# Retention out of PSUM, a scheduler that knows the shared port, and reordered blocks in a hybrid attention and retention step

## The chip, the cores and the metric

One core of a Trainium2 chip runs the whole step in one launch. The metric is the device time in microseconds (us) of an execution, as the median of several. The engines are TensorE (PE; its weight loads are PEld), VectorE (DVE), ScalarE (ACT), GpSimd (POOL) and the DMA queue that SyncE (SP) feeds. SBUF is the on-chip memory; PSUM holds the matmuls' results in banks.

## What is computed

There are 1152 tokens: 128 context tokens and 1024 latent ones, of width 1024. One layer modulates its normalised input by a condition, projects it into attention and retention operands, runs both branches, gates, merges and projects out. Cut to what matters:

```python
mod = silu(cond) @ w_mod + b_mod
shift, scale, gate = split(mod, 3)
h = layernorm(x) * (1 + scale) + shift
qa, ka, va, za, qr, kr, vr, zr = split(h @ w_in)          # 8 heads of 2 x 64 / 128, 8 heads of 64 / 128
# differential attention, per head, with rotary on latent q and k, context keys ahead
oa = (softmax(q1 k1^T / 8) - lam * softmax(q2 k2^T / 8)) @ v
oa = rmsnorm(oa) * subln_g * (1 - lam_init);  oa = (oa * silu(za)) @ w_pa
# retention, per head, once forward and once backward over chunks of 128 tokens
inner = (q k^T) * decay_in                                # inside a chunk
o = inner @ v + (q @ s) * q_dec                           # s: state from the chunks before
s = s * chunk_dec + (k * k_dec)^T @ v                     # the recursion
orr = layernorm(o_fwd + o_bwd) * ret_gn_g;  orr = (orr * silu(zr)) @ w_pr
g = sigmoid(h @ w_gate + b_gate)
out = (g_a * oa + g_r * orr) @ w_out
y = layernorm(alpha * x + gate * out) * ln_g + ln_b
```

Outputs are y for both kinds of token, the context's keys and values, and the context's final retention states.

## The kernel before

The work is laid out in stages that follow one another on every engine. A head stage (to about 100 us) computes the modulation and `Y`, the modulated input, split into a rounded high part and a low part, so that three matmuls at a time make one exact product. Stage A (to about 645 us) runs the dense projections for q, k and v of both branches (`dn` banks) while `core()` runs retention; stage B (to 1345 us) runs the softmax of the attention while the other projections and gates serve as filler; stage D (to 1648 us) projects both branches; stage E multiplies by `w_out` and normalises the output, in nine blocks of 128 tokens and two halves of 512 columns.

Within a stage, one program writes the instructions of all engines, and class `Sched` sets in which order. It keeps a clock `t` for PE, advanced by each matmul's price in `mm` (L133), and a time for each of ACT, DVE and POOL, advanced in `op` (L54) by a price per operation (`act`, `v_tt`, `v_ts`, `v_stt`, `p_tt`, `p_ts`). Streams are generators that yield the time at which their next operands will be ready; `run` (L104) asks the streams in order and lets the first that is ready issue, and dense matmuls fill what is left. The order is thus fixed when the kernel is built; each engine's instructions then run in that order and wait for one another on semaphores.

Retention, `core()` at L761: per pair of heads, PE transposes the keys, and DVE scales them into `KD`. Per head, nine matmuls give U, the chunks' updates, in three PSUM banks of the pool `a` (of four); ACT copies U to SBUF; DVE runs the recursion `SS` over seven chunks, one `scalar_tensor_tensor` forward on 64 partitions and one backward on the other 64 at each (L157). POOL makes `QD`, the decayed queries. `inner` (L818): PE multiplies q and k, DVE multiplies by the decay `DT` into `inn`. `outp` (L827): PE adds `inn` times v and `QD` times `SS` in a bank, ACT copies it to `osb`, DVE takes statistics (`stt`, `mvr`). Then POOL makes `rstd`, `norm` (L858) normalises `osb` in place on DVE, PE transposes it, and ACT copies the result to `on`. Beside all that, the projections of q and k go through the rotation: DVE makes `sw` and `rt` out of `dn`, POOL and DVE finish `rt`, ACT and POOL or DVE split it into `qkh` and `qkl`. ACT and POOL also split each weight tile into `whi` and `wlo`.

`decays()` at L652 runs at the start of `core()`: it loads the decay parameters `dec` in five small loads, `kx` and `lp`, and computes `lg`, `kdec` and `DT` from them on DVE and ACT. `phase_h` (L332) loads the modulation's weights: `wm` with a row block at a time and `wk`. `softmax_stream` (L985) first waits until `sch.t + 8`, then issues score tiles `S`; DVE takes the maximum `nm`, ACT the exponential `E`. `out_stream` (L1406) issues the blocks of stage E in order, both halves of one before the next.

Of the kernel before, what the change touches and what calls it, by code (L numbers as in the profile page):

```python
# [18 lines left out]
P = 128  # L19
# [18 lines left out]
class Sched:  # L38
# [6 lines left out]
    def __init__(self):  # L45
        self.t = 0.0
        self.e = {"act": 0.0, "dve": 0.0, "pool": 0.0}
        self.q = []
# [78 lines left out]
def hybrid_step(ctx: ExitStack, tc: tile.TileContext, I: dict, O: dict):  # L127
# [5 lines left out]
    def mm(out, lhsT, rhs, start, stop):  # L133
        n = rhs.free_size()
        sch.t += max(n / 2400, 0.107) if lhsT.dtype == F32R else max(n / 600, 0.214)
        nc.tensor.matmul(out, lhsT=lhsT, rhs=rhs, start=start, stop=stop)  # L136

    def tpose(out, in_):
        sch.t += 0.107
        nc.tensor.transpose(out, in_, ident)  # L140
# [5 lines left out]

    def v_tt(out, a, b, op, after=None):
        nc.vector.tensor_tensor(out, a, b, op=op)  # L148
        return sch.op("dve", 0.07 + out.free_size() / 960, after)

    def v_ts(out, a, s1, s2, op0, op1=None, after=None, fast=False):
        kw = {} if op1 is None else {"op1": op1}
        nc.vector.tensor_scalar(out, a, s1, s2, op0=op0, **kw)  # L153
        return sch.op("dve", 0.12 + out.free_size() / (1920 if fast else 960), after)
# [13 lines left out]
    def p_tt(out, a, b, op, after=None):  # L168
        nc.gpsimd.tensor_tensor(out, a, b, op=op)  # L169
        return sch.op("pool", 0.2 + out.free_size() * (0.17 if op == ALU.pow else 0.00205), after)  # L170

    def p_ts(out, a, s1, op0, after=None):
        nc.gpsimd.tensor_scalar(out, a, s1, None, op0=op0)  # L173
        return sch.op("pool", 0.2 + out.free_size() * 0.0013, after)
# [155 lines left out]


    def phase_h(first):  # L332
# [3 lines left out]
        with es:  # L336
# [144 lines left out]
            for k in range(0, KT, 2):  # L481
                load_wk(1, k)
            by_rows("scale", 0)
# [74 lines left out]
    def phase_a():  # L558
        es_ps = ExitStack()
        psum_pool(es_ps, "a", 4)  # L560
# [78 lines left out]
        last_parts = phase_h(first)  # L639
# [12 lines left out]
        def decays():  # L652
            rd = I["ret_decay"]
            dec = pa.tile([P, 32], F32, name="dec")
            dma(dec[:, 0:16], rd.rearrange("d h -> (d h)").partition_broadcast(P))
            rp = rd.rearrange("d (q two) -> two d q", two=2)
            for r in range(2):
                dst = dec[r * 64:(r + 1) * 64, 16:24].rearrange("p (d q) -> p d q", d=2)
                dma(dst, rp[r].partition_broadcast(64))
                dma(dec[r * 64:(r + 1) * 64, 24:32], rd[r].partition_broadcast(64))  # L660
            kx = pa.tile([P, 16], F32, name="kx")
            dma(kx, I["ret_kexp"])
            lp = pa.tile([P, 4, 64], F32, name="lp")
            dma(lp, I["lam_params"].partition_broadcast(P))
# [96 lines left out]
        def core():  # L761
# [3 lines left out]
            for p in range(4):  # L765
# [17 lines left out]
                for e in range(2):  # L783
# [8 lines left out]
                    U = pa.tile([P, NTILE, P], F32, tag="U", name="U")  # L792
# [6 lines left out]
                    for g0, gn in GR:  # L799
                        yield room("a")  # L800
                        ups, tok = psum("a", (P, 4, P))
                        for i in range(gn):
                            c = g0 + i
                            mm(ups[:, i, :], KD[e][:, c].rearrange("p d k -> p (d k)"), vr[:, c, vs], True, True)
                        tok[0] = act(U[:, g0:g0 + gn, :], ups[:, :gn, :])
                    dma(O["st"][h], U[:, NTILE - 1, :])
                    s_f = tok[0]
                    for c in range(NCH - 1):
                        b = NCH - 1 - c
                        fw, bw = (s0[0:64, :], s0[64:128, :]) if c == 0 else (SS[0:64, c, :], SS[64:128, b, :])  # L810
                        v_stt(SS[0:64, c + 1, :], fw, g128[0:64, h:h + 1], U[0:64, c, :], ALU.mult, ALU.add, s_f)
                        s_f = v_stt(SS[64:128, b - 1, :], bw, g128[64:128, h:h + 1], U[64:128, b, :], ALU.mult, ALU.add)
# [3 lines left out]
                    mv = pa.tile([P, NTILE, 2], F32, tag="mvr", name="mvr")  # L816

# [9 lines left out]
                    def outp(g0, gn, t, _):  # L827
# [7 lines left out]
                        f = act(osb[:, g0:g0 + gn, :], ops[:, :gn, :])  # L835
                        for i in range(gn):
                            v_bn(stt[:, g0 + i, :], ops[:, i, :], f)
                            nc.vector.bn_aggr(mv[:, g0 + i, :], stt[:, g0 + i:g0 + i + 1, :])
                            f2 = sch.op("dve", 0.08)
                        tok[0] = max(f, f2)  # L840
                        return f2
# [93 lines left out]
    def phase_b():  # L935
# [49 lines left out]
        def softmax_stream():  # L985
            n = 0
            yield sch.t + 8.0
# [418 lines left out]
        def out_stream():  # L1406
            for i in range(NTILE):
                ts = slice(i * P, (i + 1) * P)
# [9 lines left out]
                st, mv, rs = sm[:, 0:12].rearrange("p (g s) -> p g s", g=2), sm[:, 12:14], sm[:, 14:15]  # L1418
                for g in range(2):
                    gs = slice(g * 512, (g + 1) * 512)  # L1420
                    yield room("e")
                    ps, tok = psum("e")
                    for k in range(KT):
                        mm(ps, X[k][:, 0, ts], Y[:, 0, k, gs], k == 0, False)
                        mm(ps, X[k][:, 0, ts], Y[:, 1, k, gs], False, False)
                        mm(ps, X[k][:, 1, ts], Y[:, 0, k, gs], False, k == KT - 1)
                        if k % 2:
                            yield 0
                    tok[0] = v_tt(y[:, gs], ps, gl[:, gs], ALU.mult)
                    v_stt(y[:, gs], xt[:, gs], ALPHA, y[:, gs], ALU.mult, ALU.add)  # L1430
                    f = v_bn(st[:, g, :], y[:, gs])
# [3 lines left out]
                def fin(i=i, y=y, mv=mv, rs=rs):  # L1435
# [6 lines left out]
                sch.later(f, fin, "y")  # L1442
            done["E"] = True
# [125 lines left out]
```

## Time and profile before

| what | value |
|---|---|
| median of three runs | 1761.46 us (1760.38 to 1763.36) |
| the profiled execution's own time | 1763.77 us |
| its span | 1761.8 us |
| mean granted clock of PE | 0.981 |
| PE busy | 1676.1 us, 95% of the span |
| DVE, ACT, POOL busy | 902.6, 621.9, 819.3 us |
| moved by DMA | 237.36 MB, 135 GB/s in the mean |

The span is the profiled execution from its first to its last instruction; 2.0 us of its time lie around it. Busy time counts what an engine executes; that PE is busy says neither at which clock nor whether a matmul waited for its operands within its own record. [...]

### The profile page before, as it was taken

The page shows a single profiled execution, that of the slowest core. Times are in us where ns is not written, and L with a number is a line of the kernel's source. Part 1 is how long each engine was busy: PE and PEld are TensorE (multiplying, and loading weights), DVE is VectorE, ACT ScalarE, POOL GpSimd, SP SyncE. Part 2 cuts the span into 40 slices and gives each one's busy share as a digit, 9 for nine tenths or more (in the row PEclk, how much of TensorE's full clock was granted, in tenths as well). Part 3 has the DMA queues.
Part 4 walks back from the last instruction along what each step waited for, and adds up shares of the span by engine and source line. Part 5 has one row for each costly group of instructions (what it writes and reads, how often), then busy time and mean ns, then how long its engine had stood idle before and what let it go on. Part 6 is the DMA issues. An engine that isn't in the chain of part 4 may idle for free.

```text
span 1761.8 us, 27014 instructions
## 1 busy us (share of the span) xinstructions
PE 1676.1 (95%) x10471; PEld 1621.6 (92%) x10471; DVE 902.6 (51%) x1675; ACT 621.9 (35%) x1163; POOL 819.3 (47%) x553
## 2 busy tenths in 40 slices
PE   6989999899899989999999999999999999999997
PEld 4789899899899879999999999999999999999786
DVE  8636606612742744656565556556655013234666
ACT  5532212322222224545555555554555220012200
POOL 4636415532552645767466746575755332112211
PEclk8999999999999989999999999999999999999999
DMA  8245322330230254353535353535342568754422
GB/s 300 85 121 142 100 70 66 105 128 24 96 120 24 95 170 149 125 185 113 158 104 163 99 162 98 161 98 157 99 150 81 200 231 275 257 179 139 163 101 90
DMA packets 135040, 237.36 MB, mean 135 GB/s; under 512 B 15784, under 2 KB 103040, under 8 KB 133888
## 3 DMA queue, kind: packets, MB, share of 16 engines
q1 hardware_dynamic: 134912, 235.63, 41.4%
q8 instruction: 83, 1.36, 0.3%
q14 instruction: 45, 0.37, 0.1%
HBM read 161.08 MB, written 74.49 MB: 134 GB/s over the span
## 4 chain that ended last, share of the span: by engine, by line
PE 71%; DVE 12%; DMA 7%; issue 4%; POOL 3%; ACT 2%; SPq 1%; POOLq 0%; DVEq 0%; ACTq 0%
PE dn L136 45%; PE S L136 8%; PE o L136 5%; PE e L136 5%; PE tp L140 4%; DVE SS L157 3%; PE a L136 3%; DMA gt<-Gd 3%; DVE junk L157 2%; DMA gt<-ONd 1%; DVE osb L153 1%; SPq L187 1%; DMA lp<-in_lam_params 1%; DVE sw L598 1%; PE tp L136 1%
## 5 line engine op out<-in xcount | busy, mean ns | idle before, releaser
L136 PE MATMUL dn<-Y,whi 128*128 128x384 f32 x3200 | 837.3, 342 | 5.2 <-DVE rt L148 3.1
L136 PEld LDWEIGHTS dn<-Y,whi 128*128 128x128 f32 x3200 | 569.0, 190 | 11.3 <-DVE rt L148 4.0
L136 PE MATMUL dn<-Y,wlo 128*128 128x384 f32 x1600 | 538.1, 336 | 0.0
L169 POOL TENSOR_TENSOR wlo<-raw,whi 128x1024 fp32r<-128x1024 f32 x87 | 209.6, 2412 | 477.7 <-ACT whi L143 477.0
L136 PEld LDWEIGHTS dn<-Y,wlo 128*128 128x128 f32 x1600 | 302.2, 189 | 0.1
L1029 DVE TENSOR_REDUCE nm<-S 128x1 f32<-128x1152 f32 x144 | 178.2, 1237 | 187.3 <-PE S L136 187.2
L143 ACT ACTIVATE E<-S,nm 128x1152 f32<-128x1152 f32 x144 | 162.2, 1126 | 95.7 <-DVE nm L1029 95.4
L173 POOL TENSOR_SCALAR E<-E,r 128x640 f32<-128x640 f32 x64 | 146.4, 2287 | 93.2 <-DVE r L157 65.4
L136 PE MATMUL dn<-whi,Y 128*128 128x256 f32 x864 | 156.5, 283 | 9.5 <-DVE rt L148 7.9
L136 PEld LDWEIGHTS dn<-whi,Y 128*128 128x128 f32 x864 | 134.4, 190 | 10.5 <-ACT ln L143 8.2
L136 PE MATMUL o<-wTh,V 128*128 128x256 f32 x576 | 131.5, 287 | 0.0
L143 ACT ACTIVATE wTh<-tp 128x512 fp32r<-128x512 f32 (+1 forms) x168 | 89.5, 543 | 104.6 <-PE tp L140 103.9
L143 ACT ACTIVATE whi<-raw 128x1024 fp32r<-128x1024 f32 x88 | 91.9, 1053 | 87.3 <-PE dn L136 87.3
L136 PE MATMUL dn<-wlo,Y 128*128 128x256 f32 x432 | 121.2, 281 | 0.0
L136 PE MATMUL S<-K,QH 128*128 128x384 f32 (+1 forms) x400 | 97.2, 347 | 10.1 <-ACT E L143 6.1
L148 DVE TENSOR_TENSOR wTl<-tp,wTh 128x512 fp32r<-128x512 f32 (+1 forms) x168 | 98.1, 612 | 15.9 <-ACT wTh L143 15.9
L169 POOL TENSOR_TENSOR E<-E 128x640 f32<-128x640 f32 x64 | 100.2, 1565 | 5.3
L136 PEld LDWEIGHTS o<-wTh,V 128*128 128x128 f32 x576 | 99.2, 188 | 0.2
L136 PE MATMUL S<-K,QL 128*128 128x384 f32 (+1 forms) x400 | 93.5, 337 | 0.4 <-DMA QL<-Ql 0.4
L140 PE MATMUL tp<-ident,E 128*128 128x128 f32 x584 | 88.2, 272 | 1.8 <-DVE wTl L148 1.8
L153 DVE TENSOR_SCALAR KD<-tp,kdec 128x256 f32<-128x256 f32 (+1 forms) x48 | 16.0, 408 | 144.3 <-PE tp L140 144.3
L157 DVE SCALAR_TENSOR_TENSOR gt<-gt,dn 128x384 f32<-128x384 f32 x48 | 26.6, 554 | 120.8 <-DMA gt<-Gd 66.6
(201 smaller groups left out, 2594.4 us busy)
## 6 DMA issues: line engine op xcount, KB each, us to landing
K<-Kd SPq DMA_DIRECT2D x8, 1280.0 KB, 7.2
V<-Vd SPq DMA_DIRECT2D x24, 384.0 KB, 4.1
Gd<-gt SPq DMA_DIRECT2D x48, 192.0 KB, 2.1
gt<-Gd SPq DMA_DIRECT2D x48, 192.0 KB, 2.4
Y<-OAd SPq DMA_DIRECT2D x16, 576.0 KB, 4.9
raw<-in_w_gate SPq DMA_DIRECT2D x16, 512.0 KB, 4.8
QH<-Qh SPq DMA_DIRECT2D x64, 128.0 KB, 2.8
QL<-Ql SPq DMA_DIRECT2D x64, 128.0 KB, 2.9
```

Of the source, the lines that this page charges most:

```text
L136: nc.tensor.matmul(out, lhsT=lhsT, rhs=rhs, start=start, stop=stop)
L140: nc.tensor.transpose(out, in_, ident)
L143: nc.scalar.activation(out, in_, func, **kw)
L148: nc.vector.tensor_tensor(out, a, b, op=op)
L153: nc.vector.tensor_scalar(out, a, s1, s2, op0=op0, **kw)
L157: nc.vector.scalar_tensor_tensor(out, a, s, b, op0=op0, op1=op1, **kw)
L169: nc.gpsimd.tensor_tensor(out, a, b, op=op)
L173: nc.gpsimd.tensor_scalar(out, a, s1, None, op0=op0)
L187: nc.sync.dma_start(out=out, in_=in_)
L598: nc.vector.stream_shuffle(sw[:, :n], ps[:, :n], SWAP)
L1029: nc.vector.tensor_reduce(nm[:, m:m + 1], ps[:, :nb, :kw], axis=AX.XY, op=ALU.max, negate=True)
```

## The change

Six things are changed.

1. `Sched.op` models a port that DVE and POOL share: a DVE operation whose inputs lie in SBUF and a POOL operation don't overlap in the model; one waits for the other. PE's prices are raised a little.
2. The loads of `dec`, `kx` and `lp` are issued in `phase_h`, behind the second group of `wk` loads, into a pool of their own.
3. U stays in PSUM: the recursion reads the banks, which are held until it has ended. The context chunk's U alone is copied, to `ust`, which is stored. The order of the three groups is now the single one first.
4. The copy to `osb` is dropped: the statistics read the output banks, as before, and the norm reads them too and writes `osb`. The three banks are held until the norm has ended.
5. `softmax_stream` starts at `sch.t + 16`.
6. `out_stream` issues the first two blocks as first halves of both, then second halves of both.

The numbers of instructions are the same on PE, DVE, POOL and SP. ACT has 48 copies fewer (24 of U, 24 of `osb`) and 8 more (`ust`).

```diff
-    def op(self, eng, cost, after=None):
+    def op(self, eng, cost, after=None, port=False):
+
         s = max(self.e[eng], self.t + self.LAG if after is None else after)
+        if port:
+            other = "pool" if eng == "dve" else "dve"
+            mine, theirs = self.held[eng], self.held[other]
+            for a, b in theirs:
+                if a < s < b:
+                    s = b
+            mine.append((s, s + cost))
+            del mine[:-24]
+            if theirs and theirs[-1][0] >= s:
+                self.held[other] = [(a, b) if a < s else (a + cost, b + cost) for a, b in theirs]
+                self.e[other] += cost
         self.e[eng] = s + cost
...
-        sch.t += max(n / 2400, 0.107) if lhsT.dtype == F32R else max(n / 600, 0.214)
+        sch.t += max(n / 2400 + 0.013, 0.11) if lhsT.dtype == F32R else max(n / 600 + 0.01, 0.22)
...
+    def in_sbuf(*aps):
+        return all(a.tensor.space != PSUM for a in aps)
...
-        return sch.op("dve", 0.12 + a.free_size() / 960, after)
+        return sch.op("dve", 0.12 + a.free_size() / 960, after, in_sbuf(a, b))
...
             for k in range(0, KT, 2):
                 load_wk(1, k)
+            load_decays()
             by_rows("scale", 0)
...
-                    for g0, gn in GR:
+                    U, u_tok = {}, []
+                    for g0, gn in (GR[2], GR[0], GR[1]):
...
-                        tok[0] = act(U[:, g0:g0 + gn, :], ups[:, :gn, :])
-                    dma(O["st"][h], U[:, NTILE - 1, :])
-                    s_f = tok[0]
+                            U[c] = ups[:, i, :]
+                        if gn == 1:
+                            ust = pa.tile([P, P], F32, tag="ust", name="ust")
+                            tok[0] = act(ust, ups[:, 0, :])
+                            dma(O["st"][h], ust)
+                        else:
+                            u_tok.append(tok)
...
-                        v_stt(SS[0:64, c + 1, :], fw, g128[0:64, h:h + 1], U[0:64, c, :], ALU.mult, ALU.add, s_f)
+                        v_stt(SS[0:64, c + 1, :], fw, g128[0:64, h:h + 1], U[c][0:64], ALU.mult, ALU.add, s_f)
...
+                    for tok in u_tok:
+                        tok[0] = s_f
...
-                        f = act(osb[:, g0:g0 + gn, :], ops[:, :gn, :])
...
-                            normed[0] = v_ts(osb[:, c, :], osb[:, c, :], mv[:, c, 0:1], rstd[:, c:c + 1],
-                                             ALU.subtract, ALU.mult, fast=True)
+                            normed[0] = v_ts(osb[:, c, :], outs[c], mv[:, c, 0:1], rstd[:, c:c + 1],
+                                             ALU.subtract, ALU.mult)
+                        for tok in o_tok:
+                            tok[0] = normed[0]
...
-            yield sch.t + 8.0
+            yield sch.t + 16.0
...
+            order = [(0, 0), (1, 0), (0, 1), (1, 1)] + [(i, g) for i in range(2, NTILE) for g in range(2)]
+            for i, g in order:
+                if g == 0:
+                    begin(i)
+                yield from part(i, g)
```

Three places show how the instructions move. The helpers stand 16 lines lower now, so the same operation has another line number.

The first is SP's queue in the head stage. Before:

```order
L187 DMA wk<-in_w_scale_k 128x2x512 x4
L187 DMA wm<-in_w_shift 128x1024 x4
L187 DMA raw<-in_w_ka 128x1024
L187 DMA wm<-in_w_shift 128x1024
L187 DMA rc<-in_rope_c 128x1024
L187 DMA rsn<-in_rope_s 128x1024
L187 DMA raw<-in_w_vr 128x1024 x2
L187 DMA dec<-in_ret_decay 128x16
L187 DMA dec<-in_ret_decay 64x8x1
L187 DMA dec<-in_ret_decay 64x8
```

After:

```order
L203 DMA wk<-in_w_scale_k 128x2x512 x4
L203 DMA dec<-in_ret_decay 128x16
L203 DMA dec<-in_ret_decay 64x8x1
L203 DMA dec<-in_ret_decay 64x8
L203 DMA dec<-in_ret_decay 64x8x1
L203 DMA dec<-in_ret_decay 64x8
L203 DMA kx<-in_ret_kexp 128x16
L203 DMA lp<-in_lam_params 128x256
L203 DMA wm<-in_w_shift 128x1024 x4
L203 DMA raw<-in_w_ka 128x1024
```

Before, `dec`, `kx` and `lp` came behind the last `vr` load; they now stand behind the `wk` loads and ahead of the last five `shift` loads and of all that follows.

The second is DVE between two heads of the first pair: the norm of one (`osb`), the recursion of the next (`SS`), with the dense values' low parts `vl` between. Before:

```order
L153 TENSOR_SCALAR osb<-osb,mvr,rstd 128x128 x9
L148 TENSOR_TENSOR vl<-dn,vh 128x256
L157 SCALAR_TENSOR_TENSOR SS<-s_1391,g_628,U 64x128 x2
L148 TENSOR_TENSOR vl<-dn,vh 128x256
L157 SCALAR_TENSOR_TENSOR SS<-SS,g_628,U 64x128 x2
L148 TENSOR_TENSOR vl<-dn,vh 128x256
L157 SCALAR_TENSOR_TENSOR SS<-SS,g_628,U 64x128 x4
L148 TENSOR_TENSOR vl<-dn,vh 128x256
L157 SCALAR_TENSOR_TENSOR SS<-SS,g_628,U 64x128 x6
L598 STREAM_SHUFFLE sw<-dn 128x384
L148 TENSOR_TENSOR rt<-dn,rc 128x384
L148 TENSOR_TENSOR inn<-a,DT 128x512 x2
```

After:

```order
L164 TENSOR_TENSOR vl<-dn,vh 128x256
L169 TENSOR_SCALAR osb<-a,mvr,rstd 128x128 x9
L164 TENSOR_TENSOR vl<-dn,vh 128x256
L173 SCALAR_TENSOR_TENSOR SS<-s_1393,g_641,a 64x128 x2
L164 TENSOR_TENSOR vl<-dn,vh 128x256
L173 SCALAR_TENSOR_TENSOR SS<-SS,g_641,a 64x128 x4
L164 TENSOR_TENSOR vl<-dn,vh 128x256
L173 SCALAR_TENSOR_TENSOR SS<-SS,g_641,a 64x128 x4
L164 TENSOR_TENSOR vl<-dn,vh 128x256
L173 SCALAR_TENSOR_TENSOR SS<-SS,g_641,a 64x128 x4
L164 TENSOR_TENSOR vl<-dn,vh 128x256
L164 TENSOR_TENSOR inn<-a,DT 128x512 x2
```

The norm and the recursion now read banks of `a`, the steps are spread 2, 4, 4, 4 and not 2, 2, 4, 6, and the rotation's `sw` and `rt` no longer stand between the recursion and `inn`.

The third is ACT at the same place. Before:

```order
L143 ACTIVATE vh<-dn 128x256
L143 ACTIVATE osb<-a 128x512 x2
L143 ACTIVATE osb<-a 128x128
L143 ACTIVATE vh<-dn 128x256 x3
L143 ACTIVATE on<-tp,gng 128x512 x2
L143 ACTIVATE on<-tp,gng 128x128
L143 ACTIVATE SS<-s_1391 64x128 x2
L143 ACTIVATE U<-a 128x512 x2
L143 ACTIVATE U<-a 128x128
```

After:

```order
L156 ACTIVATE vh<-dn 128x256 x3
L156 ACTIVATE on<-tp,gng 128x512 x2
L156 ACTIVATE on<-tp,gng 128x128
L156 ACTIVATE SS<-s_1393 64x128 x2
L156 ACTIVATE ust<-a 128x128
L156 ACTIVATE vh<-dn 128x256 x4
L156 ACTIVATE nv<-dn 128x256
```

The copies of `osb` and U are gone, and `ust` has come. `on` is the copy of the transposes of the head before.

At the start of the softmax stream, PE's order has 69 dense matmuls (384 columns, `dn<-Y`) between the last retention transpose (`tp<-ident,osb`) and the first score tile (`S<-K,QH`) before, and 120 after. From the first score tile to the last, PE's order holds 2088 such dense matmuls before and 1959 after, for 144 score tiles.

## Rows read from the trace of the kernel before

**Rows 1.** Busy time by stage: stretch, length, engines, PE clock, DMA share, GB/s.

```profile
100.00:650.00 550.00, 521.55 (x3516) 509.70 (x3516) 263.61 (x605) 137.65 (x288) 247.75 (x183) 0.97 0.30 93
650.00:658.00 8.00, 3.65 (x14) 2.86 (x13) 0.00 (x0) 0.58 (x1) 0.00 (x0) 0.79 1.05 313
658.00:1345.00 687.00, 678.02 (x4397) 671.91 (x4396) 399.24 (x676) 367.18 (x700) 430.04 (x270) 1.00 0.42 134
```

**Rows 2.** Whom PE waits for, 100 to 650 us: total us, times, longest us.

```profile
PE a L136 <- DVE inn L148: 12.8, 6, 2.9
PE tp L140 <- ACT on L143: 8.2, 4, 2.9
PE dn L136 <- DVE rt L148: 3.1, 3, 2.1
```

**Rows 3.** Sum over eight stretches at clock 0.50, 217 to 628 us, as Rows 1.

```profile
sum 30.60, PE 28.51 PEld 27.63 DVE 10.22 ACT 6.42 POOL 15.06; mean PE 3.56 PEld 3.45 DVE 1.28 ACT 0.80 POOL 1.88
```

**Rows 4.** Two other stretches at the low clock, same columns.

```profile
94.80:101.60 6.80, 3.32 (x15) 3.35 (x16) 4.07 (x20) 0.46 (x3) 3.67 (x5) 0.50 0.00 0
...
654.60:661.40 6.80, 5.98 (x18) 5.50 (x19) 1.36 (x1) 1.31 (x2) 0.00 (x0) 0.50 1.07 344
```

**Rows 5.** DVE groups, 100 to 650 us: busy us, mean ns | idle before.

```profile
L157 DVE SCALAR_TENSOR_TENSOR SS<-SS,g,U 64x128 f32<-64x128 f32 x96 | 65.5, 683 | 2.5
...
L153 DVE TENSOR_SCALAR osb<-osb,mvr,rstd 128x128 f32<-128x128 f32 x72 | 32.4, 521 | 2.2 <-POOL rstd L169 2.0
L157 DVE SCALAR_TENSOR_TENSOR SS<-s,g,U 64x128 f32<-64x128 f32 x16 | 20.6, 1285 | 8.2 <-ACT U L143 8.0
...
L153 DVE TENSOR_SCALAR KD<-tp,kdec 128x256 f32<-128x256 f32 x32 | 12.9, 474 | 144.3 <-PE tp L140 144.3
```

**Rows 6.** Tile SS: operation, count: minimum/median/maximum ns, first and last start.

```profile
L157 DVE SCALAR_TENSOR_TENSOR SS<-SS,g,U x96: 334/353/2547, 157.7 to 620.0; 64x128 f32<-64x128 f32 x96
```

**Rows 7.** Timeline around one recursion: start us, length us [idle before <-releaser].

```profile
287.75 4.14 DVE L157 SCALAR_TENSOR_TENSOR SS<-SS,g,U 64x128 f32<-64x128 f32 x4
...
289.23 2.50 POOL L169 TENSOR_TENSOR wlo<-raw,whi 128x1024 fp32r<-128x1024 f32 x1 [0.24 <-ACT whi L143]
...
291.92 1.29 DVE L148 TENSOR_TENSOR inn<-a,DT 128x512 f32<-128x512 f32 x2
...
292.76 0.75 PE L136 MATMUL a<-vr,inn 128*128 128x128 f32 x2 [1.69 <-DVE inn L148]
```

**Rows 8.** The tile tz, columns as in Rows 6.

```profile
L157 DVE SCALAR_TENSOR_TENSOR tz<-tz,dn x42: 539/555/556, 696.8 to 1419.3; 128x384 f32<-128x384 f32 x42
```

**Rows 9.** Timelines of SP, DVE and PE around the decay loads.

```profile
73.05 3.32 SPq L187 DMA_DIRECT2D dec<-in_ret_decay  x5
...
91.28 0.29 DVE L148 TENSOR_TENSOR lpr<-lp 128x128 f32<-128x128 f32 x1 [8.17 <-DMA lp<-in_lam_params]
...
98.28 0.55 PE L136 MATMUL dn<-whi,Y 128*128 128x256 f32 x1 [7.93 <-DVE rt L148]
```

**Rows 10.** The stretch behind the decay loads, columns as in Rows 1.

```profile
78.60:88.60 10.00, 10.00 (x59) 10.00 (x58) 1.03 (x3) 2.02 (x3) 6.76 (x4) 1.00 0.05 1
```

**Rows 11.** Timeline: issue of four shift loads, and a reader on DVE.

```profile
31.75 12.60 SPq L187 DMA_DIRECT2D wm<-in_w_shift  x4
...
44.23 1.22 DVE L157 SCALAR_TENSOR_TENSOR junk<-wm,scb 128x1024 bf16<-128x1024 f32 x1
```

**Rows 12.** Timeline of PE: a retention transpose, and the first score tile.

```profile
638.84 0.27 PE L140 MATMUL tp<-ident,osb 128*128 128x128 f32 x1
...
655.03 1.33 PE L136 MATMUL S<-K,QH 128*128 128x384 f32 x3 [3.95 <-DMA QH<-Qh]
```

**Rows 13.** Whom PE waits for, 658 to 1345 us, columns as in Rows 2.

```profile
PE S L136 <- ACT E L143: 6.1, 4, 2.8
```

**Rows 14.** Timeline of PE at the second output block.

```profile
1657.05 0.50 PE L136 MATMUL e<-Y,K 128*128 128x512 f32 x1 [0.85 <-ACT Y L143]
1659.48 1.42 PE L136 MATMUL e<-Y,K 128*128 128x512 f32 x5 [1.93 <-POOL Y L169]
```

More of the change, by code (lines that the diff above doesn't have):

```diff
@@ L47, in __init__ @@
         self.e = {"act": 0.0, "dve": 0.0, "pool": 0.0}
+        self.held = {"dve": [], "pool": []}
         self.q = []
@@ L145, in act @@
         return sch.op("act", 0.06 + out.free_size() / 1200 + 0.09 * extra, after)
+    def in_sbuf(*aps):
+        return all(a.tensor.space != PSUM for a in aps)
     def v_tt(out, a, b, op, after=None):
         nc.vector.tensor_tensor(out, a, b, op=op)
-        return sch.op("dve", 0.07 + out.free_size() / 960, after)
+        return sch.op("dve", 0.07 + out.free_size() / 960, after, in_sbuf(a, b))
     def v_ts(out, a, s1, s2, op0, op1=None, after=None, fast=False):
@@ L329, in y_of, with load_decays, phase_h @@
         return Y[:, :, k, :]
-    def phase_h(first):
+    def load_decays(dec, kx, lp):
+        rd = I["ret_decay"]
+        dma(dec[:, 0:16], rd.rearrange("d h -> (d h)").partition_broadcast(P))
+        rp = rd.rearrange("d (q two) -> two d q", two=2)
+        for r in range(2):
+            dst = dec[r * 64:(r + 1) * 64, 16:24].rearrange("p (d q) -> p d q", d=2)
+            dma(dst, rp[r].partition_broadcast(64))
+            dma(dec[r * 64:(r + 1) * 64, 24:32], rd[r].partition_broadcast(64))
+        dma(kx, I["ret_kexp"])
+        dma(lp, I["lam_params"].partition_broadcast(P))
+    def phase_h(first, load_decays):
         es = ExitStack()
@@ L559, in phase_a @@
         es_ps = ExitStack()
+        early = es_ps.enter_context(tc.tile_pool(name="early", bufs=1))
+        dec = early.tile([P, 32], F32, name="dec")
+        kx = early.tile([P, 16], F32, name="kx")
+        lp = early.tile([P, 4, 64], F32, name="lp")
         psum_pool(es_ps, "a", 4)
@@ L638, in phase_a @@
         todo.append(qk_job("k", 0))
-        last_parts = phase_h(first)
+        last_parts = phase_h(first, lambda: load_decays(dec, kx, lp))
         es = ExitStack()
@@ L652, in decays @@
         def decays():
[L653 to L664, printed above, removed]
             dma(RE, I["ret_const"][:, 4:6])
@@ L1406, in out_stream, with begin @@
         def out_stream():
-            for i in range(NTILE):
-                ts = slice(i * P, (i + 1) * P)
+            T = {}
+            def begin(i):
                 sch.guard("y", 2)
@@ L1417, in out_stream, with part, fin @@
                 sm = pz.tile([P, CW], F32R, tag="gol", name="sm", bufs=2).bitcast(F32)
[L1418 to L1431, printed above, removed]
+                T[i] = y, xt, gl, sm[:, 0:12].rearrange("p (g s) -> p g s", g=2), sm[:, 12:14], sm[:, 14:15]
+            def part(i, g):
+                ts = slice(i * P, (i + 1) * P)
+                gs = slice(g * 512, (g + 1) * 512)
+                y, xt, gl, st, mv, rs = T[i]
+                yield room("e")
+                ps, tok = psum("e")
+                for k in range(KT):
+                    mm(ps, X[k][:, 0, ts], Y[:, 0, k, gs], k == 0, False)
+                    mm(ps, X[k][:, 0, ts], Y[:, 1, k, gs], False, False)
+                    mm(ps, X[k][:, 1, ts], Y[:, 0, k, gs], False, k == KT - 1)
+                    if k % 2:
+                        yield 0
+                tok[0] = v_tt(y[:, gs], ps, gl[:, gs], ALU.mult)
+                v_stt(y[:, gs], xt[:, gs], ALPHA, y[:, gs], ALU.mult, ALU.add)
+                f = v_bn(st[:, g, :], y[:, gs])
+                if g == 0:
+                    return
                 nc.vector.bn_aggr(mv, st)
                 f = rstd_of(rs, mv[:, 1:2], LN_EPS, f + 0.1)
-                def fin(i=i, y=y, mv=mv, rs=rs):
+                def fin():
                     for g in range(2):
```

23 lines of the change are left out of this document (13 added, 10 removed).

## Prediction

> **What bounds the kernel now.** First I read the busy time of each engine by stage [rows 1]. TensorE (PE) works nearly all the time: in the attention stage, 658 to 1345 us, it idles 687.00 - 678.02 = 9.0 us, in the retention stage before it (100 to 650 us) 550.00 - 521.55 = 28.45 us. No other engine is near its limit over a stage, so the time is PE's work, plus PE's waits, plus what PE loses at the lower clock. The change leaves the number of PE instructions as it is; it can only win back waits and clock.
>
> Second, whom PE waits for in the retention stage [rows 2]: DVE for the masked scores `inn` (12.8 us, six times), ACT for the copy of transposes `on` (8.2, four times), DVE for the rotation `rt` (3.1). The reader is to see that all three stand on engines that are idle half the time: it is their order and the length of single operations that counts.
>
> [...]
>
> Fourth, why DVE is late. The recursion's 96 + 16 steps take 683 and 1285 ns in the mean [rows 5] though their median is 353 [rows 6]; 2.5 us is the longest. [rows 7] shows one case: four steps of `SS` take 4.14 us from 287.75 while POOL has `wlo` from 289.23 for 2.50 us; the first `inn` comes at 291.92, and PE, out of filler, waits 1.69 us. Both read SBUF. DVE operations of the same kind with one PSUM operand, `tz`, spread over 720 us with POOL busy in most of it, have 539/555/556 ns as minimum, median and maximum [rows 8]: none is stretched.
>
> **The change part by part.**
>
> *Recursion from PSUM.* 112 steps: before 96 x 0.683 + 16 x 1.285 = 86.1 us; after, if none is stretched, 112 x 0.353 = 39.5. So 46.6 us of DVE go, 5.8 a head. The 24 copies of U by ACT go too, 8 small `ust` copies come, and the first step no longer waits for the copy. None of this is PE time; it is worth what PE waited for.
>
> *Norm from PSUM.* 72 operations of 521 ns = 37.5 us [rows 5]. After, the input is the output bank. The nearest rows are `KD`, the same operation from PSUM, 474 ns with 256 columns, twice as many, so 34.1 us is a bound from above; below, the recursion's 353 ns on 128 columns gives 25.4. I take 26, nearer to the row with the same columns. Either is a gain. [...]
>
> *Banks.* The price of the two edits: of four `a` banks two hold U until the recursion ends, three hold outputs until the norm. Queued behind that on PE are the next score or U matmuls, then all dense work. The order puts the next head's U behind the norm and its transposes, and 9 to 13 us of dense matmuls between U and the scores' use. An even head worked by hand, recursion 14 x 0.353 = 4.9 us plus the `sw`/`rt` pairs between, ends before its filler does. The bound is a wait like those of `inn`, 12.8/6 = 2.1 us, in each of eight heads: 17 us; below it is nothing.
>
> *Port in the scheduler, prices of PE.* No instruction changes; the places do. Retention waits and clock to win: 28.45 + 14.25 = 42.7 us, over the 13 waits of [rows 2] and a few small ones. I let one in seven survive or be replaced, 6.0 us, as an odd head starts its recursion close behind the norm before it. That leaves **36.7 us**, the largest term and the least certain. The `on` part (8.2 us) goes because ACT no longer has 48 copies queued ahead of it.
>
> *Decay loads earlier.* Before, five loads of `dec` are issued at 73.05 [rows 9], behind them the queue moves 1 GB/s for 10 us [rows 10], and DVE idles 8.17 us until `lp` is there at 91.28; the decays run, `rt` follows, PE starts again at 98.28 after 7.93 us [rows 9]. PE then has 3.32 us of work at half clock [rows 4]: 1.66. Together 9.6. After, the data are there long before; DVE could start at 91.28 - 8.17 = 83.1 and be through 7.0 us later, at 90.1, when PE runs dry at 98.28 - 7.93 = 90.35. I leave 0.6 of wait. But the slow block now stands ahead of the later `shift` loads: their issue began at 31.75, and DVE reads one at 44.23 [rows 11], 12.5 us later. The block's 10 us and 3.3 us of issue [rows 9] overfill that gap by 0.8. The cost lies between 0 (the transfers overlap) and, with the loads' own transfer on top, an estimated 3.5 us, passed on to the first dense work; I take 1.2. Head: 9.6 - 0.6 - 1.2 = **7.8**.
>
> *Start of the softmax stream.* PE idles 8.00 - 3.65 = 4.35 us [rows 1] at 650 to 658, for QH; then 5.98 us of work at half clock [rows 4], 3.0 lost. Between the last transpose (638.84) and this wait, 655.03 - 3.95 = 651.08 [rows 12], lie 69 dense matmuls, 12.2 us or 0.177 each. After, by the order, there are 120: 21.2 us. QH comes 655.03 - 638.84 = 16.2 us after the transpose; if it still does, PE has 5 us to spare. **7.3**.
>
> *Attention.* The later start and the shifted dense work leave less filler between score tiles: by the order 1959 dense matmuls and not 2088 from the first to the last, 129 x 0.177 = 22.8 us, 0.16 us a tile of 144. PE waited four times for `E`, 6.1 us in all [rows 13]. Thinner filler makes that more; nothing excludes that the port model makes it less, at most by 9.0. From -9 to +20; I take half of the row, **3.5 lost**.
>
> *Output blocks.* The second block's first half is put ahead of the first block's second, so PE need not have the columns of `Y` that ACT and POOL still split: 0.85 + 1.93 = **2.8** [rows 14]. The first blocks' other waits and the tail stay; the bounds are 0 and 2.8.
>
> Sum: 36.7 + 7.8 + 7.3 + 2.8 - 3.5 = 51.1. The profiled run took 1763.77; it becomes 1712.7. It lies 2.3 above the median of 1761.46, so the median becomes **1710**.
>
> **The rivals.**
>
> 1. *Half of the retention waits come back elsewhere*: banks held until the norm, `KD`, the rstd on POOL. For it: results of DVE and of ACT already make PE wait there [rows 2], and one late link is enough for a stretch at the low clock. Against it: 46.6 us of DVE and 48 ACT copies go. 36.7/2 = 18.4 less: 1729.
>
> 2. *Attention and the surviving waits gain too*, since the scheduler now keeps POOL's port in mind there: without the 3.5 lost, with all of the 9.0 us of idle and half of the residual 6.0 won, 1710 - 3.5 - 9 - 3 = 1694.5. For it: of those 687 us POOL works 430 and DVE 399 [rows 1], so they must cross. Against it: PE idles 1.3% there already.
>
> 3. *The change doesn't do what it says*: the recursion stays stretched, since one operand and the result are still in SBUF. Then only the head, the start, the output blocks and the ACT copies are won, some 24 us: 1738. Against it stands [rows 8], whose `tz` also has an SBUF operand and result. If attention then eats what is left, the time stays.
>
> [...]
>
> 5. *Slower*: attention's score tiles lose their cover. Place: PE's `S` behind ACT's `E`, 144 times. The filler per tile must fall below the chain of maximum and exponential; each tile would then wait. It decides from 51/144 = 0.36 us a tile; at 0.5 us it costs 72: 1710 + 72 - 3.5 = 1778. For it: filler does shrink. Against it: by 0.16 us only, and just four of 144 tiles waited.
>
> **How the numbers follow.** Forecast 0.60, by its own terms 1700 to 1722; rival 1 0.17, rival 2 0.08, rival 3 0.07, rival 4 0.04, rival 5 0.04. The range of 1693 to 1732 holds the forecast, rivals 1, 2 and 4; left out are 3, 5 and the tails of the others, under 2 in 10. A measurement of this kernel tells about 0.2%, 3.5 us, from no change. Slower: rival 5, 0.04. Same: the worst of rival 3, 0.02. Faster: 0.94.
>
> **What would show it.** In the profile after: `SS` steps with a mean below 0.40 us; `inn` and `on` under 6 us together in PE's waits of the retention stage; at most two or three low-clock stretches there; PE's wait at 90 us below 1 us and no wait at the first `S`; PE's waits for `E` within 0 to 20 us; no wait at the second output block. The forecast is wrong if PE waits for banks (`a` behind `osb`) or for `KD` in each head, if `SS` keeps a mean above 0.6, or if the attention stage grows by more than 10 us.

## The result and the profile after

The changed kernel took 1710.34 us in the median (1708.76 to 1711.82); the kernel before took 1761.5 beside it. The ratio is 0.9708 with a 95% interval of [0.9692, 0.9725]: 51 us less. Forecast were 1710 us. The profiled execution took 1710.94 us, with a span of 1709.2 and a mean granted clock of 0.992.

The windows view of the kernel before, in the stages that the events on TensorE (PE) mark, stands first; its columns are the stretch, its length, then busy time and count on PE, PEld, DVE, ACT and POOL, the granted clock, the DMA share and GB/s. The stages are: head up to the first U matmul; retention; 30 us around the first score tile; attention up to the last `o` matmul; the projections; the output.

```profile
0.00:150.60 150.60, 122.26 (x716) 107.62 (x717) 93.04 (x185) 69.33 (x115) 75.49 (x62) 0.93 0.51 172
150.60:640.00 489.40, 462.34 (x3109) 450.81 (x3108) 240.03 (x543) 114.91 (x237) 215.48 (x161) 0.97 0.27 84
640.00:670.00 30.00, 25.65 (x131) 24.86 (x131) 6.74 (x12) 7.98 (x13) 9.27 (x6) 0.89 0.76 246
670.00:1371.10 701.10, 692.12 (x4518) 685.98 (x4517) 405.93 (x697) 375.01 (x720) 436.88 (x275) 1.00 0.41 131
1371.10:1648.90 277.80, 274.24 (x1575) 271.69 (x1573) 79.20 (x135) 48.88 (x73) 59.94 (x31) 1.00 0.64 215
1648.90:1752.30 103.40, 99.17 (x433) 80.61 (x431) 72.42 (x98) 5.80 (x7) 20.86 (x20) 1.00 0.32 107
```

The same view of the changed kernel:

```profile
0.00:145.20 145.20, 122.15 (x713) 107.13 (x714) 90.35 (x184) 68.64 (x114) 74.73 (x62) 0.95 0.52 178
145.20:597.20 452.00, 450.04 (x3140) 443.56 (x3139) 185.07 (x547) 97.73 (x199) 215.67 (x161) 1.00 0.30 92
597.20:627.20 30.00, 23.14 (x117) 22.18 (x116) 3.92 (x6) 6.00 (x10) 6.24 (x4) 0.89 0.77 232
627.20:1309.30 682.10, 674.20 (x4417) 666.29 (x4416) 417.09 (x702) 370.18 (x717) 434.91 (x273) 1.00 0.41 131
1309.30:1600.20 290.90, 288.50 (x1661) 286.90 (x1660) 80.32 (x135) 52.59 (x79) 64.69 (x33) 1.00 0.64 212
1600.20:1699.60 99.40, 98.27 (x432) 80.74 (x431) 72.18 (x98) 5.83 (x7) 20.23 (x20) 1.00 0.34 112
```

The length less PE's busy time is PE's idle time. Adding half of PE's busy time in the stretches granted 0.50 of the full clock, as the prediction did [rows 3, 4], gives what a stage loses. I call it lost time. The half is an estimate, and a little high: in both traces back-to-back matmuls of 384 columns start 320 ns apart (median) where the granted clock is 0.50 and 173 ns where it is 1.00, by which 0.46 of the time is lost.

| us lost (idle + clock) | head | retention | first score tile | attention | projections | output | sum |
|---|---|---|---|---|---|---|---|
| before | 28.3 + 6.4 | 27.1 + 14.3 | 4.3 + 3.0 | 9.0 + 1.5 | 3.6 | 4.2 | 101.7 |
| after | 23.1 + 5.8 | 2.0 + 0 | 6.9 + 2.6 | 7.9 + 0 | 2.4 | 1.1 | 51.8 |
| gain | 5.8 | 39.4 | -2.2 | 2.6 | 1.2 | 3.1 | 49.9 |

The spans differ by 52.6 us, so this accounts for nearly all of it. Retention is where the time came from. Of the waits of [rows 2] none is left; PE's waits there are now these (total us, times, longest):

```profile
PE dn L149 <- ACT rt L156: 1.1, 2, 0.6
PE dn L149 <- DVE vl L164: 0.9, 1, 0.9
```

No stretch at the low clock is left in that stage [rows 3]. The recursion's steps, which [rows 5, 6] gave 683 and 1285 ns in the mean and 2547 at most, are all alike now (minimum/median/maximum ns):

```profile
L173 DVE SCALAR_TENSOR_TENSOR SS<-SS,g,a x96: 328/347/356, 147.8 to 572.5; 64x128 f32<-64x128 f32 x96
...
L173 DVE SCALAR_TENSOR_TENSOR SS<-s,g,a x16: 329/346/355, 146.5 to 562.2; 64x128 f32<-64x128 f32 x16
```

Laid over POOL's operations, the two traces show when the steps were long. Before, 50 of the 112 steps had no POOL operation beside them for more than 0.05 us, and all took 334 to 354 ns; 62 had one, and 58 of these took more than 450 ns. After, 97 of the 112 have one beside them, and none takes more than 356 ns. That the two engines share a port is the assumption of the scheduler's model; the traces show these lengths alone.

The norm, reading PSUM, is uniform too, at 402 ns and not a mean of 521:

```profile
L169 DVE TENSOR_SCALAR osb<-a,mvr,rstd x72: 391/402/412, 170.1 to 587.2; 128x128 f32<-128x128 f32 x72
```

The first score tile is where the prediction failed. PE waits 1.64 us for QH and then, at 619.55, 5.04 us for `gt`, the gate's copy on ACT, with the clock at 0.51 from 617.90 to 624.80 (last line). Timelines of SP, ACT and PE in the changed kernel, and a windows view of its low stretch:

```profile
600.84 0.75 SPq L203 DMA_DIRECT2D K<-Kd  x1
...
605.45 5.93 SPq L203 DMA_DIRECT2D V<-Vd  x4
...
612.27 7.57 SPq L203 DMA_DIRECT2D Gd<-gt  x3
```

```profile
618.92 0.58 ACT L156 ACTIVATE gt<-dn,bg 128x384 f32<-128x384 f32 x1 [15.49 <-DMA Gd<-gt]
```

```profile
612.25 0.79 PE L149 MATMUL S<-K,QH 128*128 128x384 f32 x3 [1.64 <-DMA QH<-Qh]
...
619.55 1.01 PE L149 MATMUL dn<-Y,whi 128*128 128x384 f32 x2 [5.04 <-ACT gt L156]
```

```profile
617.90:624.80 6.90, 5.25 (x16) 5.25 (x17) 0.00 (x0) 3.20 (x5) 2.37 (x1) 0.51 0.66 172
```

The reader is to see how the queue hands the delay on. SP issues K, QH and QL, then four V loads, which take it from 605.45 to 611.38, since the last of them goes out only at 610.86, after a wait of 3.4 us that the trace puts down to K's landing; the gate stores `Gd<-gt`, which save `gt` to memory, stand behind them, from 612.27. `gt` has two buffers, both unstored, so ACT's third copy waits 15.49 us for a store, until 618.92, and PE's dense work behind it, 5.04 us without a free `dn` bank, waits for that copy.

In the head, the decay loads now hold up a shift load, and a wait for `Y` on PE follows (DVE, then PE, whose last line is what is left of the wait at 90 us):

```profile
49.98 1.41 DVE L173 SCALAR_TENSOR_TENSOR junk<-wm,scb 128x1024 bf16<-128x1024 f32 x1 [5.31 <-DMA wm<-in_w_shift]
```

```profile
63.61 0.44 PE L149 MATMUL dn<-Y,whi 128*128 128x384 f32 x1 [2.48 <-ACT Y L156]
...
93.29 0.36 PE L149 MATMUL dn<-whi,Y 128*128 128x256 f32 x1 [1.59 <-DVE rt L164]
```

### The profile page after: what moved, and what is told of

Same layout as the page of the kernel before. It is cut to its first block, busy times and chain, and to the rows that moved or that the text cites. A ratio compares the mean times of both kernels' runs of the same rounds, so it can differ in the third digit from the quotient of the medians.

```text
span 1709.2 us, 26931 instructions
## 1 busy us (share of the span) xinstructions
PE 1656.7 (97%) x10471; PEld 1606.8 (94%) x10471; DVE 854.1 (50%) x1675; ACT 601.0 (35%) x1123; POOL 817.8 (48%) x553
## 4 chain that ended last, share of the span: by engine, by line
PE 81%; DVE 6%; DMA 5%; POOL 4%; issue 2%; ACT 2%; SPq 0%; POOLq 0%; DVEq 0%; ACTq 0%
PE dn L149 54%; PE S L149 7%; PE o L149 6%; PE e L149 6%; PE tp L153 4%; PE a L149 4%; DMA gt<-Gd 1%; DVE junk L173 1%; DMA wm<-in_w_shift 1%; POOL wlo L185 1%; ACT E L156 1%; PE tp L149 1%; DMA QH<-Qh 1%; POOL E L189 0%; DVE nm L1060 0%
## 5 line engine op out<-in xcount | busy, mean ns | idle before, releaser
L164 DVE TENSOR_TENSOR wTl<-tp,wTh 128x512 fp32r<-128x512 f32 (+1 forms) x168 | 99.4, 613 | 22.4 <-ACT wTh L156 22.3
```

## The experiments

The kernel before took 1761.5 to 1765.5 us in the median in the sets of runs, so kernels are compared by their ratio to it; 0.001 is 1.8 us. "Changed" is 0.9708. Where an experiment changes the scheduler's input, the order of all engines is planned anew.

| kernel | ratio [95% interval] | median us |
|---|---|---|
| PSUM parts undone | 0.9997 [0.9985, 1.0009] | 1762.36 |
| port model off | 0.9849 [0.9833, 0.9865] | 1734.67 |
| norm from SBUF | 0.9729 [0.9714, 0.9745] | 1713.87 |
| before, PSUM parts alone | 0.9743 [0.9726, 0.9760] | 1717.53 |
| start at 8 | 0.9755 [0.9736, 0.9773] | 1721.73 |
| decays behind the shift loads | 0.9681 [0.9662, 0.9699] | 1708.22 |
| V loads later | 0.9672 [0.9652, 0.9693] | 1706.80 |
| port model off, old prices | 0.9758 [0.9734, 0.9783] | 1724.19 |
| port model on, old prices | 0.9761 [0.9741, 0.9782] | 1724.29 |
| both remedies | 0.9658 [0.9636, 0.9679] | 1707.12 |
| both, start at 8 | 0.9722 [0.9700, 0.9744] | 1716.56 |
| both, start at 24 | 0.9642 [0.9621, 0.9663] | 1703.06 |

And the lost time of each, by the same stages and in the same way, from the windows view of one execution each:

| us lost | head | retention | first score tile | attention | projections | output |
|---|---|---|---|---|---|---|
| before | 34.7 | 41.4 | 7.3 | 10.5 | 3.6 | 4.2 |
| changed | 28.9 | 2.0 | 9.5 | 7.9 | 2.4 | 1.1 |
| PSUM parts undone | 27.3 | 50.1 | 7.7 | 11.1 | 3.0 | 1.1 |
| port model off | 32.8 | 5.3 | 8.5 | 19.5 | 3.4 | 1.1 |
| norm from SBUF | 29.4 | 7.4 | 5.6 | 7.5 | 2.6 | 1.1 |
| before, PSUM parts alone | 36.1 | 0.9 | 9.3 | 6.5 | 4.4 | 5.5 |
| start at 8 | 29.1 | 1.8 | 9.3 | 18.4 | 3.6 | 1.1 |
| decays behind the shift loads | 27.8 | 2.0 | 7.8 | 8.0 | 1.9 | 1.1 |
| V loads later | 29.3 | 1.5 | 1.6 | 12.4 | 2.1 | 1.1 |
| port model off, old prices | 27.4 | 0.6 | 7.9 | 17.9 | 3.5 | 1.1 |
| port model on, old prices | 28.4 | 2.6 | 8.8 | 22.3 | 3.9 | 1.1 |
| both remedies | 27.0 | 2.0 | 1.8 | 14.6 | 1.8 | 1.1 |
| both, start at 8 | 27.3 | 1.7 | 9.8 | 16.8 | 3.9 | 1.1 |
| both, start at 24 | 27.6 | 2.2 | 4.2 | 9.0 | 3.0 | 1.1 |

**PSUM reads or the scheduler's model?** Two runs take one of the two away, one adds the first alone.

```diff
# PSUM parts undone (in the changed kernel)
+                        tok[0] = act(U[:, g0:g0 + gn, :], ups[:, :gn, :])
...
+                        f = act(osb[:, g0:g0 + gn, :], ops[:, :gn, :])
```

> The changed kernel with U and the outputs copied to SBUF by ScalarE again, so that recursion and norm read SBUF; everything else, the port model too, stays. Theory (the retention gain comes from steps that no longer overlap in SBUF with GpSimd): most of it is lost, 25 to 38 us, so 1735 to 1748 us; the recursion's mean step is back above 600 ns. Rival (the gain comes from the order that the port model makes, which keeps the two engines apart by itself): at most 10 us lost, 1711 to 1720 us, mean step below 450 ns.

Measured: nothing is left of the gain, 0.9997. That is more than the theory asked for, and the rival falls. The recursion's median step is 730 ns, twice the 353 of before [rows 6], so the port model doesn't keep the two engines apart, and retention loses more than before (50.1 against 41.4). The tile `SS` in this kernel, and PE's waits in its retention stage:

```profile
L173 DVE SCALAR_TENSOR_TENSOR SS<-SS,g,U x96: 332/730/2558, 151.8 to 628.2; 64x128 f32<-64x128 f32 x96
```

```profile
PE a L149 <- DVE inn L164: 11.7, 6, 3.3
PE tp L153 <- ACT on L156: 10.6, 5, 2.9
PE tp L153 <- DVE osb L169: 7.7, 6, 2.6
```

```diff
# port model off (in the changed kernel)
-        if port:
+        if False:
```

> The changed kernel with the port model switched off in the scheduler; PSUM reads, raised TensorE prices, loads and orders stay. Theory (PSUM reads carry the gain): 1708 to 1718 us, within 8 us of the changed kernel, and the recursion's mean step stays below 360 ns. Rival (the model's order carries it): 20 us or more lost, 1730 to 1750 us, by waits for rt, qkl or the norm.

Measured: 0.9849, 25 us slower than the changed kernel. The number is the rival's, the place is not: the steps stay at 347 ns and retention loses 5.3 us, where the rival had it lost. The largest part goes in the attention stage, 19.5 against 7.9 us of lost time; the head loses 3.9 more and retention 3.3. `SS` in this kernel, then PE's waits in its attention stage, and the same waits in the changed kernel:

```profile
L173 DVE SCALAR_TENSOR_TENSOR SS<-SS,g,a x96: 328/347/357, 150.3 to 577.8; 64x128 f32<-64x128 f32 x96
```

```profile
PE S L149 <- ACT E L156: 9.2, 9, 2.3
PE o L149 <- DVE wTl L164: 8.0, 8, 1.4
```

```profile
PE S L149 <- ACT E L156: 4.8, 5, 1.6
...
PE o L149 <- DVE wTl L164: 0.9, 2, 0.5
```

The kernel before with the PSUM parts alone (the same lines as in the change, nothing else of it):

> The kernel before with only the PSUM reads of recursion and norm added; no port model, old prices, loads, start and output order. Theory: the retention waits and their clock stretches shrink by 25 to 38 us, so 1723 to 1737 us; the waits at 90 us, at the first score tile and at the second output block stay. Rival (the port model carries it): less than 10 us won, 1752 to 1761 us.

Measured: 0.9743, 45 us of the 51, more than the theory's 25 to 38. Retention loses 0.9 us, where the head, the first score tile and the output lose 1 to 2 us more than before. The windows view of its retention stage shows it; 447.0 us hold 446.1 of PE work:

```profile
152.10:599.10 447.00, 446.14 (x3123) 440.36 (x3122) 182.50 (x542) 97.30 (x198) 215.19 (x161) 1.00 0.31 92
```

So the PSUM reads carry the gain: 45 us alone, 51 as the last piece (0.9997 against 0.9708). All other edits together are worth 6 us with them and nothing without.

What no run separates is the part of the ACT copies that go with the SBUF reads. The traces speak for the reads: before, DVE waited 8.0 us for the copies of U [rows 5], and its steps were longer than now by 86.1 - 38.6 = 47.5 us; and with the 24 copies to `osb` back (the next run), PE's waits for `on` don't come back.

**The norm.** In the changed kernel only `osb` is copied again, and the norm reads it there:

```diff
+                        f = act(osb[:, g0:g0 + gn, :], ops[:, :gn, :])
...
-                            normed[0] = v_ts(osb[:, c, :], outs[c], ...
+                            normed[0] = v_ts(osb[:, c, :], osb[:, c, :], ...
```

> The changed kernel with the outputs copied to osb by ScalarE again and normalised there; the recursion still reads PSUM. Theory (the recursion is the larger part): 3 to 12 us lost, 1713 to 1722 us. Rival (a PSUM operand makes the norm slower than it would be from SBUF, 402 against 336 ns, and holds three banks, so that copying first is better): 0 to 5 us won, 1705 to 1710 us.

Measured: 0.9729, 3.7 us slower, at the theory's lower end; the intervals [0.9714, 0.9745] and [0.9692, 0.9725] overlap, so that it is slower is likely and not shown. Retention loses 7.4 and not 2.0 us, part of it given back at the first score tile. From SBUF the norm has a lower median but a long tail, 2520 ns:

```profile
L169 DVE TENSOR_SCALAR osb<-osb,mvr,rstd x72: 331/338/2520, 170.7 to 597.3; 128x128 f32<-128x128 f32 x72
```

Of these 72 norms, 14 ran beside a POOL operation and took over 1.0 us each; the other 58 took 331 to 343 ns. So beside POOL the operation that is shorter by itself is the longer one in all: 72 x 0.402 = 28.9 us from PSUM, 37.5 from SBUF before [rows 5].

**The start of the softmax stream.**

```diff
# start at 8 (in the changed kernel)
-            yield sch.t + 16.0
+            yield sch.t + 8.0
```

> The changed kernel with the softmax stream starting at 8 instead of 16. Theory of the prediction (the later start gives QH time to land, worth 7.3 us with its clock): 5 to 9 us lost, 1715 to 1720 us. Rival, from the trace of the changed kernel, where TensorE still waits 1.6 us for QH and then 5.0 us for the gate copy gt (the transfers, not the start, set this place): within 3 us, 1707 to 1714 us.

Measured: 0.9755, 8.3 us slower. The theory had the size and not the place. At the first score tile, the lost time is the same with either start, 9.3 and 9.5 us: with 8, PE waits for QH, with 16 for the gate's copy. The difference lies in the attention stage, 18.4 against 7.9. PE's waits at the first score tile, then in the attention stage, with the start at 8:

```profile
PE S L149 <- DMA QH<-Qh: 6.9, 1, 6.9
```

```profile
PE S L149 <- ACT E L156: 7.9, 7, 1.8
PE o L149 <- DVE wTl L164: 3.8, 4, 2.2
```

```diff
# V loads later (in the changed kernel)
             used = 0
+            yield sch.t + 12.0
             for _ in range(4):
                 load_v()
```

> The changed kernel with the first four V loads issued 12 us of the scheduler's time later, so that on the DMA queue the gate stores Gd stand ahead of them. Theory (V loads share the memory with K and QH and hold the gate stores back, so TensorE waits 1.6 us for QH and 5.0 us for gt and then runs at a low clock): 5 to 10 us won, 1700 to 1706 us, no wait for gt. Rival (K's own 1.28 MB set the time, or the low clock comes anyway): under 2 us, 1708 to 1711 us.

Measured: 0.9672, 6.3 us faster, as the theory had it, though the two intervals, [0.9652, 0.9693] and [0.9692, 0.9725], just meet. The lost time at the first score tile falls from 9.5 to 1.6 us, and PE's waits there are these; so the V loads ahead of the gate stores were the cause.

```profile
PE dn L149 <- ACT gt L156: 0.9, 1, 0.9
PE S L149 <- DMA QL<-Ql: 0.7, 1, 0.7
```

Attention gave 4.5 of it back, 12.4 against 7.9, and the trace shows where: 20 us behind the first score tile PE waits 3.14 us for `E` (then 3.4 us of work at half clock, 1.7 lost), since ACT's order has a `gt` ahead of that `E`, and this `gt` waits 6.83 us for a gate store again. ACT, then PE:

```profile
627.50 0.58 ACT L156 ACTIVATE gt<-dn,bg 128x384 f32<-128x384 f32 x1 [6.83 <-DMA Gd<-gt]
627.98 1.21 ACT L156 ACTIVATE E<-S,nm 128x1152 f32<-128x1152 f32 x1
```

```profile
629.34 0.79 PE L149 MATMUL S<-K,QH 128*128 128x384 f32 x3 [3.14 <-ACT E L156]
```

**The decay loads.**

```diff
# decays behind the shift loads (in the changed kernel)
-            load_decays()
             by_rows("scale", 0)
...
+        load_decays(dec, kx, lp)
         dma(rc, I["rope_c"])
```

> The changed kernel with the decay loads issued behind all shift loads and ahead of rc, that is later than in the change and earlier than before. Theory (the decay block delays the shift loads: DVE waits 5.3 us for one at 50 us, TensorE 2.5 us for Y at 61 us with a low clock behind it): 2 to 5 us won, 1705 to 1709 us, and DVE's wait for wm is gone. Rival (the shift loads are not on the path, the head is bound by the conditioning work on DVE): within 1.5 us of 1710.

Measured: 0.9681, 4.8 us faster by ratio, though the two intervals, [0.9662, 0.9699] and [0.9692, 0.9725], overlap. DVE's wait for `wm` is gone, and PE's longest wait for `Y` falls from 2.5 to 1.1 us, though its waits for `Y` add up to as much as before (4.2 us against 3.7); the lost time shows 1.1 us less in the head and 1.7 at the first score tile. The head's lost time differs by 2.1 us between kernels whose head has the same order (27.3 with the PSUM parts undone, 29.4 with the norm from SBUF), so the gain can't be placed, and that the shift loads were worth it isn't shown.

**Prices and model.**

> The changed kernel with the port model off and TensorE's prices as before, so the scheduler of before with the new PSUM reads, loads, start and output order. The kernel with the model off alone took 1734.7 us, the one with PSUM reads alone 1717.5. Theory (the raised prices without the model harm the attention stage): 1710 to 1718 us. Rival (the later start harms it when the model is off): 1728 to 1738 us.

The edit: the model off, as above, and the old `mm` and `tpose` prices. Measured: 0.9758, between theory and rival; its executions spread from 1716.75 to 1724.84 us, and the profile is of the shortest. The old prices win 16 us over the raised ones with the model off, but attention still loses 17.9.

> The changed kernel with TensorE's prices as before, the port model on. With the model off, the old prices were 16 us better than the raised ones. Theory A (raised prices are wrong by themselves for the attention stage): 5 to 16 us better than the changed kernel, 1694 to 1705 us. Theory B (model and prices only fit together): 0 to 15 us slower, 1710 to 1725 us, by waits in the attention stage.

Measured: 0.9761, 9 us slower than the changed kernel, so theory A falls: raised prices are not wrong by themselves. The loss is in attention again, 22.3 against 7.9:

```profile
PE S L149 <- ACT E L156: 10.6, 7, 3.2
```

In the changed kernel, attention loses 19.5 us with the raised prices alone, 22.3 with the model alone and 7.9 with both. But with neither it loses 17.9 here and 6.5 in the kernel before with the PSUM parts, where start, loads and output order are the old ones. So neither model nor prices make this stage good or bad by themselves. What in the order does it was not found. It isn't the amount of filler: between the first and the last score tile stand 1959 dense matmuls of 384 columns in the changed kernel (7.9 us lost), 1983 with the start at 8 (18.4), 2076 with the model off (19.5), 2088 with the PSUM parts alone (6.5) and 2091 with the old prices (22.3).

**Both remedies, and the start again.**

> The changed kernel with both remedies: the decay loads behind the shift loads, and the first V loads 12 us later. Alone they won 4.8 and 6.4 us by ratio. Theory (two places, two causes): they add up, 10 to 12 us below the changed kernel, 1698 to 1702 us, no long wait for gt and none for wm. Rival (each only shifts where the stages meet): under 8 us, 1703 to 1708 us.

Measured: 0.9658, 8.8 us below the changed kernel and between the two guesses; the lost time is 1.8 us at the first score tile, but 14.6 in attention, 6.4 of it in a wait for `E` at 628.68 and a clock of 0.51 from 628.0 to 634.9, as with the V loads alone.

> Both remedies with the softmax stream starting at 8. In the changed kernel the start at 8 cost 8.3 us by ratio, but in its trace 10.5 of them lie in the attention stage, not at the start. Theory A (the later start is worth something at its own place, where QH must land): 5 to 9 us slower than with both remedies alone, the loss within 15 us of the first score tile. Theory B (the start number only throws the attention stage's order into another one, better or worse by chance): the loss, if any, lies later, where TensorE waits for E and wTl.

Measured: 0.9722, 11 us slower than both remedies at 16. That is more than theory A's 5 to 9, but now the place is theory A's: 8.0 of it are lost at the first score tile (9.8 against 1.8), where PE waits for QH again, and 2.2 in attention:

```profile
PE S L149 <- DMA QH<-Qh: 7.1, 1, 7.1
```

> Both remedies with the softmax stream starting at 24. Theory A (a later start only helps until QH is there, which 16 already allows): within 2 us of both remedies at 16. Theory B (the order of the attention stage is thrown anew): 3 to 10 us off in either direction, in waits for E and wTl.

Measured: 0.9642, 2.8 us better than at 16 with overlapping intervals, so the two theories aren't told apart. Against the changed kernel, 0.9708 [0.9692, 0.9725], it is 11.6 us faster, the fastest of all: 1703.06 us. Attention loses 9.0.

## Why the prediction was right, and where it was not

The time was met to 0.4 us, but only with luck: errors of its terms cancel. One by one:

- **Retention, 36.7 forecast, 39.4 measured.** Right, and by the mechanism named: steps of 347 ns (0.353 forecast), norms of 29 us in all (26), `inn` and `on` gone from PE's waits, no low clock. The 6.0 us set aside for surviving waits were too many; 2.0 are lost. The prediction booked this term under the scheduler's port and prices; the run with the PSUM parts alone, at 40.5, shows that it needs neither. The 14.25 us that the sum has for the clock are half of the 28.51 us of [rows 3], and that half no run shows: the matmul starts of 320 and 173 ns make it 13.1. After the change no stretch of the stage is below full clock.
- **Head, 7.8 forecast, 5.8 measured.** PE's wait for `rt` at 91 us fell from 7.93 to 1.59, not to 0.6. The shift loads were held up as feared, but by 5.31 us on DVE, above the bound of 3.5: from the issue of `dec` at 30.90 to the landing of `lp` at 48.71 the block took 17.8 us and not the 13.3 that [rows 9, 10] had given. PE took 2.48 us of that. And 2.3 of the 5.8 aren't the change's: they are a shorter wait for `rows` at 36 us (6.73 before, 4.42 after), which is 4.2 to 6.8 in kernels whose head has the same order.
- **First score tile, 7.3 forecast, -2.2 measured.** The step that failed is "QH comes 16.2 us after the transpose; if it still does". QH came 612.25 - 589.52 = 22.7 us after it; on SP's queue its load (601.70) follows the last query's store, `Qh<-qkh` (599.81), and the load of K (600.84), which takes 10.0 us to land. And the wait that went was replaced: with the start at 16, the gate's copy waits for its store behind the V loads, which [rows 12] couldn't show and the order of SP's queue could. The run with V loads later won 7.9 us at this place and lost 4.5 by the same queue 20 us on.
- **Attention, 3.5 lost forecast, 2.6 won measured.** Wrong in sign, and the reason given, thinner filler, falls with it (the counts above). The gain isn't the port model's either: with the PSUM parts alone this stage loses 6.5. Given the raised prices, the model is worth 11.6 here.
- **Output blocks, 2.8 forecast, 3.1 measured.** Right; every kernel with the new order loses 1.1 us there.

The first-tile term was 9.5 us too high and the head 2.0, the attention term 6.1 too low and retention 2.7; the projections gave 1.2 that had no term, and the output 0.3 more. That made the sum fit. Of the signs named, the mean step (0.345 us), the end of `inn` and `on` and the absence of low-clock stretches in retention came as said; the waits at 90 us (1.59, not below 1) and at the first `S` (1.64, not none) did not.

**The rivals.** Rival 1 (half of the retention waits come back) fell: 2.0 us are lost. That one late link is enough for a low clock held in the trace of before for some waits and not for others: the 1.69 us until 292.76 [rows 7] were followed by 3.4 us at 0.50, those of 2.04 until 313.97 and of 1.63 until 472.16 by 9.4 and 15.6 us at 1.00. Rival 2 (attention gains its whole idle time) had the direction; 7.9 of 9.0 us stayed. Rival 3 (steps still stretched by the SBUF operand and result) fell with a maximum of 356 ns; [rows 8] had said so. Rival 4 (slow PSUM operands): for the norm, there was a price, 402 ns against a median of 336 from SBUF before:

```profile
L153 DVE TENSOR_SCALAR osb<-osb,mvr,rstd x72: 332/336/2500, 178.4 to 637.5; 128x128 f32<-128x128 f32 x72
```

The two-input steps show no penalty at all, 347 from PSUM against 353. Where the norm's 66 ns come from, at one length of 128 columns, no run tells. Copying its operand to SBUF first, for one operation, left the kernel 3.7 us slower by the ratios, with overlapping intervals.

Rival 5 had its mechanism in sight: with the model alone or the raised prices alone, PE does wait for `E` and `wTl` 15 to 20 us in all, but 144 tiles each waiting was far off.

The steps took up to 2547 ns with two SBUF inputs and at most 356 with one. That POOL is held in its turn doesn't show here: it is busy for 215.5 us of the retention stage before and 215.7 after.

## What to carry to other kernels

Reading a matmul's result straight from PSUM was worth far more here than the instruction's own length says: the norm's median even grew, from 336 to 402 ns, yet the PSUM reads alone were worth 45 us: DVE's steps beside POOL went from as much as 2547 ns to 356 at most, and PE, which waits behind them, lost 0.9 us to waits and clock in the retention stage and not 41.4. A term for a wait that goes has to name what is late next on the same queue and at the same place; here a store behind loads took over at once. And a scheduler's model and its prices have to be changed and measured together: taking away either one alone made the attention stage worse. That stage lost between 6.5 and 22.3 us in the plans tried here, and the cause was not found, so a gain of that size in one plan doesn't show that the edit works.

## What was not expected of the hardware

The median step of the recursion from SBUF was 353 ns in one order and 730 in another, with the same instructions: 62 of the 112 steps met a POOL operation in one, 73 in the other. And the small loads of `dec`, `kx` and `lp`, 17.8 us from the first issue to the last landing, held up the 512 KB loads queued behind them for so long that DVE stood still for 5.31 us. SP itself stood still for 3.8 us, until a `dec` load had landed, before it issued the third of them; why the small loads take so long, no run here shows.
